# RWKV chunk solve: seven dependent 32-row steps per chunk, or a 128x128 inverse completed on TensorE and one product

## The chip, the cores and the metric

One core of a Trainium2 chip. The metric is the device time of one execution in microseconds, as the median of several runs.

## The reference, cut to what matters

Two transformer-like blocks on 256 tokens of width 2048. The first block mixes tokens by a Mamba-2 SSD on one half of the heads and by RWKV-7 on the other, then comes a cross-attention and an MLP; the second block has window attention, an S5 scan and a gated MLP. The RWKV-7 mixer, with 16 heads of 64, is the part at hand:

```
def step(state, inp):
    r_t, w_t, k_t, v_t, kk_t, a_t = inp
    sa = jnp.einsum('bhij,bhj->bhi', state, -kk_t)
    state = (state * w_t[:, :, None, :] + sa[..., None] * (kk_t * a_t)[:, :, None, :]
             + v_t[..., None] * k_t[:, :, None, :])
    return state, jnp.einsum('bhij,bhj->bhi', state, r_t)
```

Both kernels compute it in two chunks of 128 tokens. Inside a chunk the recurrence over `sa` becomes a unit lower triangular system of 128 unknowns per head: (I - G) z = b, with G strictly triangular.

## The kernel before, in words

All large products (`gemm`) stream fp32 weights from HBM in units of 1024 columns per partition. SyncE issues the loads; ScalarE rounds a unit to fp32r (`wh`), VectorE takes the rest (`wl`), and TensorE multiplies weight and activation halves in fp32r, into banks of the pool `mm` (four banks in this phase). The order of the large products is `w_in`, `wk`, `wv`, `w_outa`, `w_outb`, and so on.

Everything else is side work: Python generators that `step` resumes between groups of weight products. A hand-made meter (`Meter`) estimates the engines' time; a generator is resumed when its own time has come, so each `yield` is a hop of at least one group. What is emitted so is then ordered per engine by a planner that simulates the program; each engine works through its instructions in order. `step(True)` (forced) is called where a product needs a result of side work that is not there.

The RWKV side work of eight head pairs i (two heads in one 128-partition tile), in four quarters of two pairs:

- `rwkv_prep(i)`: scaled tiles `ka`, `be`, `al`, `rh`, `vt`, `bon` (pool `g`, 42 tiles) and `ga`, the masked 128x128 matrices G of two heads and two chunks. It holds back while `i > outs + LIVE`, where `outs` counts finished pairs.
- `rwkv_inv(q)`: GpSimd gathers the four 32x32 diagonal blocks of eight matrices (two pairs, two heads, two chunks), VectorE transposes them, GpSimd inverts all of them in 31 steps (tiles `T` and `W`), VectorE transposes the result into `Wc`. One at a time. Its tiles come from a pool of three.
- `rwkv_out(i)`, up to four at once: per chunk, products `gkp`, right side `b`, then the solve by forward substitution over four row blocks: the update `c` (from the second block on) and the product `z` with the block's inverse, each with its evacuation by VectorE and a `yield`; then state `s0` and result `y`. At the end it loads the second half of the pair's `lora` by SyncE into the tile `kbt` and writes its result into `bon`, which becomes `mix[8 + i]`.

The weight product `wv` has four blocks of two banks; `evac_v` writes four tiles per block, blocks 0 and 1 into the pool `m` (35 tiles), blocks 2 and 3 into the pool `g`. `w_outb` needs all of `mix`.

Of the kernel before, what the change touches and what calls it, by code (L numbers as in the profile page):

```python
# [13 lines left out]
AF = mybir.ActivationFunctionType  # L14
ALU = mybir.AluOpType
AX = mybir.AxisListType
P = 128
# [284 lines left out]
class Net:  # L302
# [116 lines left out]
    def step(self, force=False):  # L419

        mt, keep = self.meter, self.meter.t
        if force and self.sides:
            mt.clk["pe"] = max(mt.now(), min(e[0] for e in self.sides))
        for e in list(self.sides):
            if e[0] <= mt.now():
                mt.t = max(e[0], mt.now())
                try:
                    next(e[1])
                    e[0] = mt.t + e[2]
                except StopIteration:  # L430
                    self.sides.remove(e)
        mt.t = keep
# [267 lines left out]
    def rwkv_inv(self, qn, qd):  # L700

        nc = self.nc
        gp = nc.gpsimd
        iv = lambda n: self.ivp.tile([P, 1024], F32, tag="iv", name=f"{n}{qn}")
        Dt = iv("D")
        gp.memset(Dt, 0.0)
        d3 = Dt.rearrange("p (c h) -> p c h", h=32)
        for i in (2 * qn, 2 * qn + 1):
            for h in range(2):
                for q in range(4):  # L710
                    s = slice(32 * q, 32 * q + 32)
                    o = (i % 2) * 4 + 2 * h
                    gp.tensor_copy(d3[s, :, o:o + 2].rearrange("p c h -> p h c"),
                                   qd[i]["ga"][h].rearrange("p (c t) -> p c t", c=2)[s, :, 32 * q:32 * q + 32])
        for _ in range(3):
            yield
        L = iv("L")
        nc.vector.transpose(L, Dt)
        W = iv("W")
        T = self.ivp.tile([P, 256], F32, tag="ivt", name=f"T{qn}", bufs=1)  # L720
        nc.sync.dma_start(W, self.io["eye32"])
        w3 = W.rearrange("p (c i) -> p c i", i=32)
        for k in range(31, 0, -1):
            n = 32 - k
            t3 = T[:, :n * k].rearrange("p (c i) -> p c i", i=k)
            self.mul(t3, L[:, 32 * k:32 * k + k].unsqueeze(1).broadcast_to((P, n, k)),
                     w3[:, k:, k:k + 1].broadcast_to((P, n, k)), gp)
            self.add(w3[:, k:, :k], w3[:, k:, :k], t3, gp)
        for _ in range(13):
            yield  # L730
        Wc = iv("Wc")
        nc.vector.transpose(Wc, W)
        qd["wc"] = Wc.rearrange("p (c h) -> p c h", h=32)

    def rwkv_out(self, i, qd):
        nc = self.nc
        st = qd[i]
        ka, be, al, rh, vt, ga, nn, wc = (
            st["ka"], st["be"], st["al"], st["rh"], st["vt"], st["ga"], st["nn"], qd["wc"])
        hq = (i % 2) * 4  # L740

        yt = ka
        h64 = lambda h: slice(64 * h, 64 * h + 64)
        pt = self.pst(f"kt{i}")
        nc.tensor.transpose(pt[:, :P], ka[:, :P], self.ident)
        nc.tensor.transpose(pt[:, P:S], be[:, :P], self.ident)
        kbt = self.gp.tile([P, S], F32, tag="kb", name=f"kbt{i}", bufs=KB)
        self.act(kbt[:, :P], pt[:, :P], AF.Copy)
        self.mul(kbt[:, P:].rearrange("p (h j) -> p h j", h=2), pt[:, P:S].rearrange("p (h j) -> p h j", h=2),
                 nn[:, 0:2].unsqueeze(2).broadcast_to((P, 2, 64)))  # L750
        s0 = None
        for c in range(2):
            cc = slice(c * P, (c + 1) * P)
            gks = []
            pts = self.pst2(f"gkp{i}{c}")
            self.beside([(pts[h][:, n * P:(n + 1) * P], a[h64(h), cc], b[h64(h), cc], True, True)
                         for n, (a, b) in enumerate(((ka, rh), (ka, al), (be, rh))) for h in range(2)])
            for h in range(2):
                gk = self.t2(f"gk{i}{c}{h}")
                pt = pts[h]  # L760
                self.mul(gk[:, :S], pt[:, :S], self.c("mk"))
                self.stt(gk[:, S:3 * P], pt[:, S:3 * P], nn[:, 2 * c + h:2 * c + h + 1], self.c("mk", 0, P), ALU.mult, ALU.mult)
                gks.append(gk)
            yield
            pt = self.pst(f"b{i}{c}")
            if c:
                nc.tensor.matmul(pt[:, :P], al[:, cc], s0, start=True, stop=False)
            for h in range(2):
                nc.tensor.matmul(pt[:, h64(h)], gks[h][:, P:2 * P], vt[:, c * P + 64 * h:c * P + 64 * h + 64],
                                 start=c == 0, stop=c == 0 or h == 1)  # L770
            b, z = be[:, cc], al[:, cc]
            self.act(b, pt[:, :P], AF.Copy)
            yield
            for q in range(4):
                rows = slice(32 * q, 32 * q + 32)
                if q:
                    pt = self.pst(f"c{i}{c}{q}")
                    for h in range(2):
                        nc.tensor.matmul(pt[rows, h64(h)], ga[h][:32 * q, c * P + 32 * q:c * P + 32 * q + 32],
                                         z[:32 * q, h64(h)], start=True, stop=True)  # L780
                    self.add(b[rows], b[rows], pt[rows, :P])
                    yield
                pt = self.pst(f"z{i}{c}{q}")
                for h in range(2):
                    nc.tensor.matmul(pt[rows, h64(h)], wc[rows, :, hq + 2 * h + c], b[rows, h64(h)], start=True, stop=True)
                nc.vector.tensor_copy(z[rows], pt[rows, :P])
                yield
            if c == 0:
                pt = self.pst(f"s{i}")
                nc.tensor.matmul(pt[:, :P], kbt[:, P:], z, start=True, stop=False)  # L790
                nc.tensor.matmul(pt[:, :P], kbt[:, :P], vt[:, :P], start=False, stop=True)
                s0 = self.t(f"s0{i}")[:, :P]
                nc.gpsimd.memset(s0, 0.0)
                for h in range(2):
                    self.ts(s0[h64(h), h64(h)], pt[h64(h), h64(h)], st["sc"][h64(h)], None, ALU.mult)
            pt = self.pst(f"y{i}{c}")
            if c:
                nc.tensor.matmul(pt[:, :P], rh[:, cc], s0, start=True, stop=False)
            for h in range(2):
                o = pt[:, h64(h)]  # L800
                nc.tensor.matmul(o, gks[h][:, :P], vt[:, c * P + 64 * h:c * P + 64 * h + 64], start=c == 0, stop=False)
                nc.tensor.matmul(o, gks[h][:, S:3 * P], z[:, h64(h)], start=False, stop=c == 0 or h == 1)
            self.act(yt[:, cc], pt[:, :P], AF.Copy)
            yield
        lo = kbt
        nc.sync.dma_start(lo, self.io["lora"][i][:, S:])
        lws = self.split(lo, f"lorg{i}")
        bs = self.small(f"bs{i}", 24)
        mv = self.small(f"mv{i}", 8)
        for j in range(4):  # L810
            nc.vector.bn_stats(bs[:, 6 * j:6 * j + 6], yt[:, 64 * j:64 * j + 64])
        for j in range(4):
            nc.vector.bn_aggr(mv[:, 2 * j:2 * j + 2], bs[:, 6 * j:6 * j + 6])
        var = self.small(f"var{i}", 4)
        self.ts(var, mv.rearrange("p (j k) -> p j k", k=2)[:, :, 1], 64e-5, None, ALU.add)
        rs = self.rsqrt_small(var, 4, f"gn{i}")
        for j in range(4):
            y = yt[:, 64 * j:64 * j + 64]
            self.ts(y, y, mv[:, 2 * j:2 * j + 1], rs[:, j:j + 1], ALU.subtract, ALU.mult)
        yield  # L820
        pt = self.pst(f"yT{i}")
        for c in range(2):
            nc.tensor.transpose(pt[:, c * P:(c + 1) * P], yt[:, c * P:(c + 1) * P], self.ident)
        for a in range(2):
            self.hilo(pt[:, S:], [w[:, a * P:(a + 1) * P] for w in lws], self.pg[a], a == 0, a == 1)
        y3, bon = self.t(f"y3{i}"), st["bon"]
        self.act(y3, pt[:, :S], AF.Identity, scale=self.v("ln_w", i), bias=self.v("ln_b", i))
        self.add(bon, y3, bon)
        self.mul(bon, bon, pt[:, S:])
        y3 = bon  # L830
        self.mix[8 + i] = y3
        self.outs += 1
        yield
# [956 lines left out]
```

## Time and profile before

| | |
|---|---|
| median of 3 runs | 2951.19 us (2949.64 to 2951.55) |
| profiled execution | 2947.2 us, span 2945.4 us |
| busy: TensorE, VectorE, ScalarE, GpSimd | 2879.7, 2066.4, 1411.1, 350.7 us |
| matmul records | 19604 |

A busy TensorE is not TensorE at its peak: matmuls overlap, so what one costs is read from the distance between starts. Each fp32 matmul of the solve leaves two records. Nearly all instructions carry the line of one recording helper, so they are told apart by the tiles that they write and read (`z<-be,Wc` writes z and reads be and Wc). The granted clock is 1.0 at 2.4 GHz and 0.5 at 1.2 GHz.

### The profile page before, as it was taken

How to read it: one execution, taken by the hardware profiler on the slowest of the kernel's cores; microseconds unless marked ns; L12 is line 12 of the kernel's file. 1: busy time of each engine (PE TensorE's matmuls, PEld its weight loads, DVE VectorE, ACT ScalarE, POOL GpSimd, SP SyncE). 2: the span in 40 equal slices, each digit the busy share in tenths (PEclk: the TensorE clock that was granted, in tenths of full speed). 3: DMA queues.
4: the chain of work that ended last, by engine and by line, in shares of the span. 5: the costliest groups of instructions: out<-in, count | busy, mean ns of one | idle time of the engine just before them, and what ended most of it. 6: DMA issues, size and time to landing. Idle time of an engine off the chain costs nothing.

```text
span 2945.4 us, 50103 instructions
## 1 busy us (share of the span) xinstructions
PE 2879.7 (98%) x19604; PEld 2618.0 (89%) x19604; DVE 2066.4 (70%) x3761; ACT 1411.1 (48%) x2223; POOL 350.7 (12%) x574
## 2 busy tenths in 40 slices
PE   8989999989999999999999989999999999999998
PEld 7988998779999989988988989999988888888887
DVE  7978777567667675565566688897767765567755
ACT  6553543324554554455455544553554444444444
POOL 3446115600000000000000051210000000000000
PEclk9999999969999999999999999999999999999999
DMA  6544544416555666666656644545565566655664
GB/s 213 176 146 126 155 147 134 155 52 192 173 152 165 185 192 188 186 187 190 191 184 186 193 141 148 157 151 172 187 192 187 182 190 187 192 186 184 189 190 146
DMA packets 146252, 504.15 MB, mean 171 GB/s; under 512 B 16352, under 2 KB 24800, under 8 KB 146016
## 3 DMA queue, kind: packets, MB, share of 16 engines
q1 hardware_dynamic: 146016, 500.96, 54.6%
q8 instruction: 153, 2.51, 0.3%
q14 instruction: 83, 0.68, 0.1%
HBM read 498.80 MB, written 2.10 MB: 170 GB/s over the span
## 4 chain that ended last, share of the span: by engine, by line
PE 86%; POOL 7%; DVE 4%; issue 2%; ACT 1%; DMA 1%; SPq 0%; DVEq 0%; POOLq 0%; ACTq 0%
PE mm_w_up L266 17%; PE mm_w_in L266 12%; PE mm_w L266 12%; PE mm_w2a L266 5%; PE mm_w_db L266 4%; PE mm_w_da L266 4%; PE mm_w2c L266 4%; PE mm_w2b L266 4%; PE mm_wo L266 3%; PE mm_wq L266 3%; POOL T L266 3%; PE mm_w_out L266 3%; POOL W L266 3%; PE mm_wk L266 2%; PE mm_w_outa L266 2%
## 5 line engine op out<-in xcount | busy, mean ns | idle before, releaser
L266 PE MATMUL mm_w_up<-xu,wh_w_up 128*128 128x512 f32 x1408 | 487.9, 397 | 0.0
L266 PE MATMUL mm_w_up<-xu,wl_w_up 128*128 128x256 f32 x1408 | 376.6, 280 | 0.0
L266 PE MATMUL mm_w<-xf,wh_w 128*128 128x512 f32 x1024 | 350.6, 392 | 0.0
L266 DVE TENSOR_TENSOR wl_w_up<-raw_w_up,wh_w_up 128x1024 fp32r<-128x1024 f32 x176 | 215.4, 1224 | 148.2 <-ACT wh_w_up L266 147.4
L266 PEld LDWEIGHTS mm_w_up<-xu,wh_w_up 128*128 128x128 f32 x1408 | 256.9, 188 | 54.7
L266 ACT CAST wh_w_up<-raw_w_up 128x1024 fp32r<-128x1024 f32 x176 | 184.8, 1050 | 236.0 <-PE mm_w_up L266 220.8
L266 ACT CAST wh_w_in<-raw_w_in 128x1024 fp32r<-128x1024 f32 (+1 forms) x189 | 196.7, 1043 | 209.8 <-PE mm_w_in L266 121.1
L266 PE MATMUL mm_w_in<-ins,wh_w_in 128*128 128x256 f32 (+1 forms) x1248 | 288.9, 318 | 6.2 <-DVE ins L266 6.2
L266 DVE TENSOR_TENSOR wl_w_in<-raw_w_in,wh_w_in 128x1024 fp32r<-128x1024 f32 (+1 forms) x189 | 241.9, 1284 | 60.1 <-ACT wh_w_in L266 58.6
L266 PEld LDWEIGHTS mm_w_up<-xu,wl_w_up 128*128 128x128 f32 x1408 | 265.6, 189 | 9.8
L266 PE MATMUL mm_w<-xf,wl_w 128*128 128x256 f32 x1024 | 273.4, 280 | 0.0
L266 PE MATMUL mm_w_in<-xb,wh_w_in 128*128 128x256 f32 x1472 | 268.6, 284 | 1.1 <-DVE in L266 1.1
L266 DVE TENSOR_TENSOR wl_w<-raw_w,wh_w 128x1024 fp32r<-128x1024 f32 x128 | 156.8, 1225 | 122.1 <-ACT wh_w L266 120.5
L266 PEld LDWEIGHTS mm_w_in<-xb,wh_w_in 128*128 128x128 f32 x1472 | 226.8, 190 | 5.7 <-issue 2.3
L266 PEld LDWEIGHTS mm_w_in<-ins,wh_w_in 128*128 128x128 f32 x1248 | 208.8, 195 | 18.6 <-DVE ins L266 6.2
L266 PEld LDWEIGHTS mm_w<-xf,wh_w 128*128 128x128 f32 x1024 | 186.8, 188 | 35.9
L266 PE MATMUL mm_w_in<-ins,wl_w_in 128*128 128x256 f32 x768 | 216.2, 289 | 2.2 <-DVE wl_w_in L266 2.1
L266 PE MATMUL mm_w_in<-xb,wl_w_in 128*128 128x256 f32 x736 | 206.4, 284 | 2.1 <-DVE wl_w_in L266 2.1
L266 ACT CAST wh_w<-raw_w 128x1024 fp32r<-128x1024 f32 x128 | 134.3, 1049 | 144.4 <-PE mm_w L266 119.1
L266 PEld LDWEIGHTS mm_w<-xf,wl_w 128*128 128x128 f32 x1024 | 192.3, 188 | 7.0
L266 PEld LDWEIGHTS mm_w_in<-ins,wl_w_in 128*128 128x128 f32 x768 | 149.8, 195 | 6.8 <-DVE wl_w_in L266 3.8
L266 POOL TENSOR_TENSOR tt<-st,st 128x256 f32<-128x256 f32 x16 | 13.8, 860 | 1112.6 <-DVE acc L266 1111.8
(1504 smaller groups left out, 7501.9 us busy)
## 6 DMA issues: line engine op xcount, KB each, us to landing
raw_w_in<-in_w_in_dram SPq DMA_DIRECT2D x187, 512.0 KB, 3.6
raw_w_up<-in_w_up_dram SPq DMA_DIRECT2D x176, 512.0 KB, 3.8
raw_w<-in_w_dram SPq DMA_DIRECT2D x128, 512.0 KB, 4.2
raw_w2a<-in_w2a_dram SPq DMA_DIRECT2D x48, 512.0 KB, 3.9
raw_w_da<-in_w_da_dram SPq DMA_DIRECT2D x44, 512.0 KB, 4.0
raw_w_db<-in_w_db_dram SPq DMA_DIRECT2D x42, 512.0 KB, 3.9
raw_w2b<-in_w2b_dram SPq DMA_DIRECT2D x40, 512.0 KB, 4.2
raw_w2c<-in_w2c_dram SPq DMA_DIRECT2D x40, 512.0 KB, 4.2
```

The lines of the kernel that those rows point to most:

```text
L266: return f(o, *a, **k)
```

## The change

`rwkv_inv` goes on after `Wc`. It copies the blocks' inverses out (`Md`) and transposes them (`MdT`); then, for all eight matrices at once and in four stages with a `yield` between, TensorE forms the off-diagonal blocks: `ia` and `ib` those of 32x32 beside two diagonal blocks, `ic` and `id` the one of 64x64. ScalarE, VectorE and GpSimd copy the parts into two more tiles of the pool of three, `Q` and `M`; `M` ends as eight 128x128 inverses. `rwkv_out` then has one product per chunk and head (`inv` times `b`), one copy and one `yield` where it had seven steps. In `step`, a forced step now always advances the meter to the next time that lies ahead of it, where it stayed if some generator was due already.

```diff
--- before.py
+++ after.py
@@ -420,7 +420,7 @@
 
         mt, keep = self.meter, self.meter.t
         if force and self.sides:
-            mt.clk["pe"] = max(mt.now(), min(e[0] for e in self.sides))
+            mt.clk["pe"] = min([e[0] for e in self.sides if e[0] > mt.now()], default=mt.now())
         for e in list(self.sides):
             if e[0] <= mt.now():
                 mt.t = max(e[0], mt.now())
@@ -730,13 +730,54 @@
             yield
         Wc = iv("Wc")
         nc.vector.transpose(Wc, W)
-        qd["wc"] = Wc.rearrange("p (c h) -> p c h", h=32)
+
+
+        Q, M = iv("Q"), iv("M")
+        j3 = lambda a, n: a.rearrange("p (j c) -> p j c", c=n)
+        m3 = j3(M, P)
+        gp.memset(M, 0.0)
+        gp.memset(Q[:64, 512:], 0.0)
+        Md, MdT, Y1, Z64 = Q[:, :256], Q[:, 256:512], T, Q[:, 512:]
+        d, z64 = j3(Md, 32), j3(Z64, 64)
+        nc.vector.tensor_copy(d, Wc.rearrange("p (c h) -> p h c", h=32)[:, :8])
+        nc.vector.transpose(MdT, Md)
+        yield
+        blk = [slice(32 * q, 32 * q + 32) for q in range(4)]
+        lo, hi = slice(0, 64), slice(64, P)
+        gs = [qd[i]["ga"][h][:, c * P:(c + 1) * P] for i in (2 * qn, 2 * qn + 1) for h in range(2) for c in range(2)]
+        c32 = [slice(32 * j, 32 * j + 32) for j in range(8)]
+        c64 = [slice(64 * j, 64 * j + 64) for j in range(8)]
+        pts = self.pst2(f"ia{qn}")
+        self.beside([(pts[q // 2][blk[q + 1], c32[j]], gs[j][blk[q], blk[q + 1]], MdT[blk[q], c32[j]], True, True)
+                     for j in range(8) for q in (0, 2)])
+        self.act(Y1[blk[1]], pts[0][blk[1], :256], AF.Copy)
+        nc.vector.tensor_copy(Y1[blk[3]], pts[1][blk[3], :256])
+        for q in range(4):
+            self.act(m3[blk[q], :, blk[q]], d[blk[q]], AF.Copy)
+        for q in range(2):
+            gp.tensor_copy(z64[blk[q], :, blk[q]], j3(MdT, 32)[blk[q]])
+        yield
+        pts = self.pst2(f"ib{qn}")
+        self.beside([(pts[q // 2][blk[q], c32[j]], Y1[blk[q + 1], c32[j]], Md[blk[q + 1], c32[j]], True, True)
+                     for j in range(8) for q in (0, 2)])
+        self.beside([(pts[0][blk[1], c32[j]], Md[blk[1], c32[j]], Y1[blk[1], c32[j]], True, True) for j in range(8)])
+        self.act(z64[blk[1], :, blk[0]], j3(pts[0][blk[1], :256], 32), AF.Copy)
+        nc.vector.tensor_copy(m3[blk[0], :, blk[1]], j3(pts[0][blk[0], :256], 32))
+        nc.vector.tensor_copy(m3[blk[2], :, blk[3]], j3(pts[1][blk[2], :256], 32))
+        yield
+        pt = self.pst(f"ic{qn}")
+        self.beside([(pt[hi, c64[j]], gs[j][lo, hi], Z64[lo, c64[j]], True, True) for j in range(8)])
+        self.act(Z64[hi], pt[hi], AF.Copy)
+        yield
+        pt = self.pst(f"id{qn}")
+        self.beside([(pt[lo, c64[j]], Z64[hi, c64[j]], m3[hi, j, hi], True, True) for j in range(8)])
+        nc.vector.tensor_copy(m3[lo, :, hi], j3(pt[lo], 64))
+        qd["inv"] = m3
 
     def rwkv_out(self, i, qd):
         nc = self.nc
         st = qd[i]
-        ka, be, al, rh, vt, ga, nn, wc = (
-            st["ka"], st["be"], st["al"], st["rh"], st["vt"], st["ga"], st["nn"], qd["wc"])
+        ka, be, al, rh, vt, nn, inv = (st["ka"], st["be"], st["al"], st["rh"], st["vt"], st["nn"], qd["inv"])
         hq = (i % 2) * 4
 
         yt = ka
@@ -771,20 +812,11 @@
             b, z = be[:, cc], al[:, cc]
             self.act(b, pt[:, :P], AF.Copy)
             yield
-            for q in range(4):
-                rows = slice(32 * q, 32 * q + 32)
-                if q:
-                    pt = self.pst(f"c{i}{c}{q}")
-                    for h in range(2):
-                        nc.tensor.matmul(pt[rows, h64(h)], ga[h][:32 * q, c * P + 32 * q:c * P + 32 * q + 32],
-                                         z[:32 * q, h64(h)], start=True, stop=True)
-                    self.add(b[rows], b[rows], pt[rows, :P])
-                    yield
-                pt = self.pst(f"z{i}{c}{q}")
-                for h in range(2):
-                    nc.tensor.matmul(pt[rows, h64(h)], wc[rows, :, hq + 2 * h + c], b[rows, h64(h)], start=True, stop=True)
-                nc.vector.tensor_copy(z[rows], pt[rows, :P])
-                yield
+            pt = self.pst(f"z{i}{c}")
+            for h in range(2):
+                nc.tensor.matmul(pt[:, h64(h)], inv[:, hq + 2 * h + c], b[:, h64(h)], start=True, stop=True)
+            nc.vector.tensor_copy(z, pt[:, :P])
+            yield
             if c == 0:
                 pt = self.pst(f"s{i}")
                 nc.tensor.matmul(pt[:, :P], kbt[:, P:], z, start=True, stop=False)
```

## Rows read from the trace of the kernel before

**Rows 1.** page: busy us of TensorE; its clock per fortieth of the span

```profile
PE 2879.7 (98%) x19604; PEld 2618.0 (89%) x19604; DVE 2066.4 (70%) x3761; ACT 1411.1 (48%) x2223; POOL 350.7 (12%) x574
PEclk9999999969999999999999999999999999999999
```

**Rows 2.** stretches: us; busy PE, PEld, DVE, ACT, POOL; clock, DMA, GB/s

```profile
40.00:500.00 460.00, 443.89 (x3482) 413.84 (x3481) 369.89 (x786) 222.68 (x412) 182.67 (x306) 0.98 0.48 149
500.00:594.07 94.07, 91.08 (x473) 71.57 (x472) 56.22 (x107) 31.31 (x41) 47.13 (x74) 0.99 0.48 150
594.07:643.58 49.51, 44.36 (x286) 37.51 (x284) 29.77 (x128) 6.01 (x19) 0.00 (x0) 0.60 0.04 14
643.58:718.87 75.29, 75.29 (x548) 68.48 (x548) 54.30 (x124) 33.88 (x52) 0.00 (x0) 0.98 0.59 182
```

**Rows 3.** timeline of PE (start, us, what): solve steps of pair 4, first chunk

```profile
547.76 0.44 PE L266 MATMUL z<-be,Wc 32*32 32x64 f32 x4
...
551.64 0.41 PE L266 MATMUL c<-al,ga 32*32 32x64 f32 x4
...
587.84 0.38 PE L266 MATMUL s<-al,kbt 128*128 128x128 f32 x2
```

**Rows 4.** groups of PE, 594.07 to 643.58: count, busy us, mean ns, idle before

```profile
L266 PE MATMUL z<-be,Wc 32*32 32x64 f32 x72 | 9.8, 290 | 0.9 <-ACT be L266 0.7
...
L266 PE MATMUL c<-al,ga 32*32 32x64 f32 (+2 forms) x48 | 6.5, 289 | 0.4 <-DVE al L266 0.4
```

**Rows 5.** timeline of DVE: `wv` evacuations, and out 5's last row between

```profile
553.82 1.28 DVE L266 TENSOR_SCALAR v<-mm_wv,memy 128x256 f32<-128x256 f32 x3
...
624.95 0.41 DVE L266 TENSOR_TENSOR bon<-bon,yT 128x256 f32<-128x256 f32 x1
...
641.47 0.88 DVE L266 TENSOR_SCALAR v<-mm_wv,memy 128x256 f32<-128x256 f32 x2
```

**Rows 6.** chain of waits (start, us, what): `w_outb`, weight products alone

```profile
718.87 46.09 PE mm_w_outb L266 x384
```

**Rows 7.** timeline of PE: one z step among weight products

```profile
306.41 0.28 PE L266 MATMUL mm_w_in<-ins,wl_w_in 128*128 128x256 f32 x1
306.62 0.44 PE L266 MATMUL z<-be,Wc 32*32 32x64 f32 x4
306.98 0.50 PE L266 MATMUL mm_w_in<-ins,wh_w_in 128*128 128x256 f32 x2
307.32 0.28 PE L266 MATMUL mm_w_in<-ins,wl_w_in 128*128 128x256 f32 x1
```

**Rows 8.** timeline of PE: z and c interleaved (first of seven rows), what follows

```profile
309.93 0.26 PE L266 MATMUL z<-be,Wc 32*32 32x64 f32 x1
...
310.30 0.39 PE L266 MATMUL mm_w_in<-ins,wl_w_in 128*128 128x256 f32 x1
```

**Rows 9.** timeline of PE: four `b` records and what follows

```profile
302.72 0.56 PE L266 MATMUL b<-vt,gk 128*128 128x64 f32 x4
303.12 0.39 PE L266 MATMUL xt<-cst,xbc 128*128 128x128 f32 x2
```

**Rows 10.** groups of the whole span: the solve steps on PE and DVE

```profile
L266 PE MATMUL z<-be,Wc 32*32 32x64 f32 x256 | 29.7, 247 | 0.9 <-ACT be L266 0.7
...
L266 PE MATMUL c<-al,ga 32*32 32x64 f32 (+2 forms) x192 | 21.1, 239 | 3.2 <-DVE al L266 3.2
...
L266 DVE COPY al<-z 32x128 f32<-32x128 f32 x64 | 18.3, 286 | 20.8 <-PE z L266 17.7 <-PE c L266 1.9
...
L266 DVE TENSOR_TENSOR be<-be,c 32x128 f32<-32x128 f32 x48 | 13.8, 287 | 18.6 <-PE c L266 16.8 <-PE z L266 0.8
```

**Rows 11.** waits, 40 to 719: who for whom, us, times, longest us

```profile
PE st L266 <- DVE xe L266: 7.0, 1, 7.0
...
PE c L266 <- DVE al L266: 3.2, 2, 2.8
...
DVE Wc L266 <- POOL W L266: 22.8, 4, 7.8
```

## The prediction

> **What bounds the kernel now.** I read the page first: TensorE is busy 98% of the span, and the slices of its granted clock show one dip, to 0.6, in the ninth [rows 1]. So time can only come from what TensorE executes, from the places where it stands still, and from that dip. Only about the first 720 us hold the RWKV work, so next I read busy times by stretch [rows 2]. From 40 to 594 us TensorE idles 19 us in 554 and runs near its full clock; 594.07 to 643.58 differs: a mean clock of 0.60 (of the two levels, 2.4 GHz at 1.0 and 1.2 GHz at 0.5, it is mostly at the lower), ScalarE 6.0 us busy, and 14 GB/s of weights where 149 to 182 flow around it. Its 44.4 us of TensorE are stretched by the clock and hold little work. The stretch after it is dense again. Call it the hole: 49.5 us without the weight product `wv`, save two records.
>
> Why is it there? In it run the outs of head pairs 4 to 7, a step at a time [rows 4]. The solve of one chunk is seven products that follow each other, each resumed only when the hand-made meter steps the side work: for pair 4 the first stands at 547.76, the second at 551.64, and the product behind the seventh at 587.84, so 40 us for seven hops [rows 3]. Meanwhile block 1 of `wv` has evacuated three of its four tiles at 553.82; the next ones come only at 641.47, after outs 4 and 5 have written their last rows (the second at 624.95) [rows 5]. By the code, blocks 2 and 3 of `evac_v` take tiles of the pool `g`, 42 in all: four finished results, eight for each of four open pairs, and the split second loads of `lora` (two tiles each) leave none. So block 2 sits in PSUM, block 3 has no bank, and TensorE has nothing but the serial solve. The link from pool to wait is inferred; the times are read.
>
> **Part 1: small products that go, outside the hole.** All z and c groups together are 256 and 192 records [rows 10], two per matmul, four per step. The hole holds 72 and 48 [rows 4], so 328 records, 82 steps, stand among weight products. What a step costs there is read from the starts around one: alone, 384 records of 256 columns take 46.09 us, 0.12 from start to start [rows 6]. Here the weight record at 306.41 is followed by z at 306.62 (0.09 late), z by the next pair at 306.98 (0.36), and that pair takes 0.34 for 0.24 (0.10 late) [rows 7]. Sum 0.55. **82 x 0.55 = 45 us go.**
>
> **Part 2: the hole.** If the outs need one hop where they needed seven, outs 4 and 5 save six hops of about 5.7 us in the first chunk alone, 34 us before the hole begins, and the pairs before them save too, which opens preparations 5 to 7 (held back by `outs + LIVE`) and the next inverse earlier. They would be through before block 2 needs tiles. Then the hole's other 164 records (286 less 120 and two of `wv`) run among weight products; four `b` records take 0.40 us [rows 9], 0.10 each, so 16 us. **49.5 - 16.4 = 33 us go.** Ends: 42, if they pack as in [rows 8] (0.046 each); 16, if the hole stays and loses only the busy time of its z and c (9.8 + 6.5, [rows 4]).
>
> **Part 3: the one product.** 16 groups of two 128-row matmuls with 64 columns, four records, like `b`: 0.40 [rows 9] and 0.19 for going in and out [rows 7]. **16 x 0.6 = 10 us come.**
>
> **Part 4: completing the inverse.** Per quarter 56 matmuls, 112 records: `ia` 32 and the first half of `ib` 32, alternating between two disjoint row groups; 16 each in the second half of `ib`, `ic` and `id`, all on one row group. For the first kind the row is z and c interleaved: eight records from 309.93 to 310.30, 0.046 each [rows 8]. For the second, z alone, 0.36 for four [rows 7], 0.09 each. So 64 x 0.046 + 48 x 0.09 + 5 insertions x 0.19 = 2.9 + 4.3 + 1.0 = 8.2 us, **33 us come in four quarters.** Ends: 25, if all pack; 62, if every four records pay the whole 0.55.
> The Trainium skill ("TensorE: Matmul & The Clock Gate", Part 3: Packing small matmuls) says that a weight load overlaps running matmuls only where the row group differs, which speaks against `ic`, `id` and half of `ib`. The two prices just read, 0.046 and 0.09, agree. Its span model, some 4 ns for each further tile, would put `ia` and the first half of `ib` near 0.4 us each where I take 1.5; as an estimate from that page the forecast would be 9 us lower.
>
> **Part 5: waits.** VectorE waits in all four quarters for GpSimd's last W, 22.8 us in sum, because it is in line behind the transpose [rows 11]. What is queued behind it is the splitting of weights, and TensorE pays later: 7.0 in its longest wait, 3.2 in others. Now `d`, its transpose and `ia` stand right behind that transpose, and TensorE is itself in order: behind `ia` are weight products. Nothing in the trace shows a TensorE wait directly on the inverse. Bounds: minus 10 (today's waits of 7.0 and 3.2 go) to plus 28 (four of 7.0). Steps that wait for an evacuation today lose little: 3.2 us in all c groups [rows 11], 0.9 in all z groups [rows 10]; so I take **1 us per quarter, 4 us come.**
>
> **At nothing.** VectorE loses 112 small operations, 32.1 us [rows 10], and gets 16 copies of like size and per quarter five small copies and a transpose, some 3 us (an estimate from 0.29 for 128 columns); ScalarE gets seven small copies, GpSimd two memsets and two copies per quarter. GpSimd is idle in half of 500 to 594 [rows 2], VectorE is under 81% from 40 to 500; if that cover failed it would show in the fourth rival. No DMA is added; each out's second `lora` load moves forward in SyncE's queue with its out, and weights behind it wait less. The line in the forced step changes only the order of emission; it also acts after 767 us, and I put plus or minus 3 us on it, an estimate: it can act only where a product waits for side work, and TensorE idles 66 us in the whole span (2945.4 - 2879.7, [rows 1]).
>
> **Sum:** -45 - 33 + 10 + 33 + 4 = -31. The profiled execution (2947.2 us, span 2945.4) would come to 2916; it lies 4 us under the median of the runs shown, so of 2951.2 I make **2920 us**.
>
> **Rivals.**
> (a) The hole stays. `g` tiles bind later too, or the planner puts the outs no earlier. For: at 641.47 the evacuation came 16 us after the last row of out 5, so the freed tile was not all [rows 5]. Against: 40 us per solve is so much the longest item. Then -45 - 16 + 10 + 33 + 4 = -14: 2937 us.
> (b) More than forecast: all stages pack (25 for 33) and today's waits of 10 us go where I add 4: -45 - 33 + 10 + 25 - 10 = -53: 2898 us. For: the first kind of stage packs already; VectorE gets lighter, so the queues behind the transpose are shorter.
> (c) Slower. TensorE's queue stops at the inverse: `ia` is placed where the planner expects W, W is late as it is in four of four quarters, and `ib`, `ic`, `id` each wait for copies on two loaded engines while weight products stand behind. At 7.0 for `ia` and 2.8 (the larger of c's two waits, [rows 11] for their sum) for three stages this is 15.4 us per quarter, 62 in all, in place of 4: +27, 2978 us. It decides from 9 us per quarter on, where the other terms (-35) are used up. Against: z and c stages, built alike, wait 4 us over 448 records.
> (d) It doesn't do what it says: the chain gets shorter but VectorE takes over as the bound. All of 40 to 719 holds 510 us of VectorE [rows 2]; the outs of 500 to 700 pulled into a stage that is 80% full would starve the weight products. If TensorE's idle 16 us of 40 to 500 doubled, and as much came in 500 to 594, it is 30 us back: 2950 us.
>
> **Chances.** Forecast 0.55 (own range 2905 to 2937), (a) 0.13, (b) 0.17, (c) 0.10, (d) 0.05. About 0.2%, 6 us, is what a measurement of this kernel tells from no change; some of (a) and of the dear end of part 4 fall within it: faster 0.82, same 0.07, slower 0.11. The range leaves out (c), part of (d), and what of (b) and of the bounds goes beyond 2893: 2893 to 2947.
>
> **What would show it.** No stretch of 40 us or more without weight products and at a clock near 0.6 before `w_outb`; `wv` blocks 1 to 3 evacuated in turn; `w_outb` begins near 687 instead of 719. z as 64 records of 128 rows; 448 records in `ia` to `id` at 0.05 to 0.1 us from start to start. VectorE's wait for W still four times. Wrong would be: TensorE waits on `ia` to `id` over 9 us per quarter, or the hole moved elsewhere with another pool full.

## The result, and the profile after

The changed kernel takes 2920.1 us (median of 4 runs, 2918.8 to 2921.0) against 2951.4 of the kernel before on the same chip; the ratio is 0.9895, with a 95% interval of 0.9877 to 0.9912. That is 31 us, or 1.05%, less. The forecast was 2920, so its sum came out. Its terms didn't all: this part of the document is mostly about that. One of the ten executions of a run further down (the stages issued three times) took 6831.9 us and is left out of that run's median.

The profiled execution of the changed kernel has a span of 2917.7 us, 27.7 less than before. The page, as in [rows 1], gives busy time, and the granted clock per fortieth of the span:

```profile
PE 2840.0 (97%) x19668; PEld 2598.8 (89%) x19668; DVE 2037.5 (70%) x3689; ACT 1423.4 (49%) x2251; POOL 357.4 (12%) x590
...
PEclk9999999999999999999999999999999999999999
```

TensorE is busy 39.7 us less (2879.7 before), with 64 records more. The dip of the clock in the ninth slice is gone.

The stretches of [rows 2], cut at the same times, in the changed kernel (columns as there: us; busy PE, PEld, DVE, ACT, POOL; clock, DMA share, GB/s), and under them the last part cut finer:

```profile
40.00:500.00 460.00, 434.57 (x3626) 413.54 (x3627) 362.18 (x793) 236.24 (x443) 187.51 (x321) 0.97 0.47 149
500.00:594.07 94.07, 88.04 (x477) 72.91 (x478) 52.59 (x94) 31.27 (x42) 48.63 (x76) 0.96 0.45 146
594.07:643.58 49.51, 49.51 (x408) 44.78 (x408) 34.52 (x81) 24.53 (x36) 0.00 (x0) 1.00 0.64 203
643.58:718.87 75.29, 71.37 (x575) 69.29 (x575) 52.88 (x143) 30.90 (x58) 0.00 (x0) 0.93 0.38 125
...
680.00:700.00 20.00, 16.08 (x104) 15.24 (x103) 12.84 (x59) 6.54 (x16) 0.00 (x0) 0.76 0.20 61
```

Three things are to be seen here. The hole is filled: 594 to 644 has TensorE busy throughout, at full clock, and 203 GB/s of weights. TensorE idles more before it: 25.4 us of 40 to 500 (16.1 before), 6.0 of 500 to 594 (3.0 before). And a new gap stands where none was: 680 to 700, clock 0.76, 61 GB/s.

What that gap is, the chain of waits shows (start, us, what):

```profile
691.79 0.64 PE mm_w_outb L266 x3
692.43 0.65 PE yT L266 x3
693.10 2.63 DMA xin<-in_x_dram
695.82 0.43 DVE xin L266
696.30 40.73 PE mm_w_outb L266 x321
```

The product `w_outb` took 46.09 us in one piece before [rows 6]. Now its first record is at 676.8 and 63 of the 384 go early, but the other 321 run from 696.30, behind the ends of outs 6 and 7 (their last `bon` rows start at 690.3 and 696.2, their last products on TensorE, `yT`, stand in this chain): 60 us from its first to its last record. In the gap TensorE falls to the lower of its two clock levels: behind 692.4 its records start 0.21 us apart, where 0.12 is usual. The very last release is a tile `xin`, loaded only at 693.10. It is the eighth of sixteen: by the code it lies in the pool `m`, and in the built program it takes the place of a tile that the products `yT` of every out read, up to the last. So this load waits for out 7 too, and SyncE's waits show it (who for whom: us, times, longest):

```profile
SPq L1548 <- PE yT L266: 8.0, 1, 8.0
```

The end of `w_outb` moved from 764.96 (718.87 + 46.09) to 737.03 (696.30 + 40.73), 27.9 us earlier, about the whole change of the span. So everything that the change did to the time it did before 740 us.

The inverse of the first quarter on TensorE, in its timeline (start, us, what), and one product of the solve with what follows it:

```profile
217.91 0.69 PE L266 MATMUL ia<-Q,ga 32*32 32x32 f32 x32
218.53 0.38 PE L266 MATMUL mm_w_in<-ins,wh_w_in 128*128 128x256 f32 x1
...
230.89 0.60 PE L266 MATMUL ib<-Q,T 32*32 32x32 f32 x26
...
231.92 0.38 PE L266 MATMUL pb<-qh,bonesr 128*128 128x256 f32 x1
...
242.78 1.14 PE L266 MATMUL ic<-Q,ga 64*64 64x64 f32 x16
243.85 0.39 PE L266 MATMUL mm_w_in<-ins,wh_w_in 128*128 128x256 f32 x1
...
248.07 1.14 PE L266 MATMUL id<-M,Q 64*64 64x64 f32 x16
...
263.69 0.55 PE L266 MATMUL z<-be,M 128*128 128x64 f32 x4
264.08 0.61 PE L266 MATMUL b<-vt,gk 128*128 128x64 f32 x4
```

From the start of a stage to the start of what follows: `ia` 0.62 us for 32 records, `ib` 1.03 for 48, `ic` 1.07 for 16, and `id` the same 1.1. That is 3.8 us, with some 0.2 for going in and out of each stage 4.6 us a quarter, where the forecast had 8.2.

The waits from 40 to 719 us (who for whom: us, times, longest), as in [rows 11]:

```profile
DVE Wc L266 <- POOL W L266: 38.8, 4, 11.9
...
PE b L266 <- DVE gk L266: 20.8, 3, 8.9
...
PE st L266 <- DVE xe L266: 7.7, 1, 7.7
```

VectorE waits 16 us more for GpSimd's W, and a wait of TensorE is new: `b`, the right side of a chunk, for `gk`. VectorE's timeline shows why (in brackets: idle before, and what ended it):

```profile
570.45 1.25 DVE L266 STREAM_TRANSPOSE Wc<-W 128x1024 f32<-128x1024 f32 x1 [10.57 <-POOL W L266]
571.61 1.18 DVE L266 TENSOR_TENSOR wl_wv<-raw_wv,wh_wv 128x1024 fp32r<-128x1024 f32 x1
572.72 0.41 DVE L266 TENSOR_TENSOR gk<-gkp,cst 128x256 f32<-128x256 f32 x1
...
573.19 1.28 PE L266 MATMUL b<-vt,gk 128*128 128x64 f32 x4 [6.03 <-DVE gk L266]
```

VectorE stands 10.57 us for W, everything behind the transpose is late by that, `gk` among it, and TensorE, which is in order as well, stands 6.03 us at `b` (the last row is TensorE's). Each of the four waits for W has such a wait of TensorE behind it: `st` at 175.2 (7.7 us), `b` at 305.5, 451.0 and 573.2 (5.9, 8.9, 6.0), 28.5 us in sum. And each costs more than it lasts: behind it TensorE goes on for a while at the lower of its two clock levels (columns of the stretches as above):

```profile
175.00:179.00 4.00, 3.78 (x19) 3.81 (x20) 4.00 (x9) 3.80 (x9) 1.71 (x3) 0.56 0.55 168
305.50:308.00 2.50, 2.50 (x15) 2.38 (x17) 2.50 (x7) 1.07 (x4) 0.00 (x0) 0.50 0.03 7
451.00:454.00 3.00, 3.00 (x14) 3.00 (x15) 2.09 (x5) 0.28 (x1) 0.62 (x1) 0.50 0.10 10
573.20:577.00 3.80, 3.80 (x19) 3.18 (x19) 3.80 (x8) 0.28 (x1) 0.00 (x0) 0.50 0.62 174
```

In the first of them the records start 0.21 us apart up to 178.5, which loses some 1.3 us (an estimate: 2.9 us of records at 0.21 in place of 0.12).

### The profile page after: what moved, and what is told of

Same layout as the page of the kernel before. It is cut to its first block, busy times and chain, and to the rows that moved or that the text cites. A ratio compares the mean times of both kernels' runs of the same rounds, so it can differ in the third digit from the quotient of the medians.

```text
span 2917.7 us, 50239 instructions
## 1 busy us (share of the span) xinstructions
PE 2840.0 (97%) x19668; PEld 2598.8 (89%) x19668; DVE 2037.5 (70%) x3689; ACT 1423.4 (49%) x2251; POOL 357.4 (12%) x590
## 4 chain that ended last, share of the span: by engine, by line
PE 78%; DVE 3%; POOL 1%; issue 1%; ACT 0%; DMA 0%; DVEq 0%; ACTq 0%; POOLq 0%
PE mm_w_up L266 17%; PE mm_w L266 12%; PE mm_w_in L266 7%; PE mm_w2a L266 5%; PE mm_w_db L266 4%; PE mm_w_da L266 4%; PE mm_w2c L266 4%; PE mm_w2b L266 4%; PE mm_wo L266 3%; PE mm_wq L266 3%; PE mm_w_out L266 3%; PE mm_wv L266 2%; PE mm_w_outa L266 2%; PE mm_w_outb L266 2%; PE mm_w_ba L266 2%; PE mm_wk L266 1%
```

## The experiments

The kernel before took 2949.1 to 2950.1 us (medians) beside the runs that follow, and 2951.4 beside the changed kernel: differences between runs of different sets are good to some 2 us. Unless it is said otherwise, times are medians of three rounds.

### The forced step, and ga held longer

The one line in the forced step, put into the kernel before:

```diff
-            mt.clk["pe"] = max(mt.now(), min(e[0] for e in self.sides))
+            mt.clk["pe"] = min([e[0] for e in self.sides if e[0] > mt.now()], default=mt.now())
```

> The kernel before with the one new line of the forced step and nothing else. The prediction put it at nothing, plus or minus 3 us: 2951, between 2948 and 2954. A rival reading of the result, that part of the 31 us is owed to this line because it moves the outs, expects 2940 or less.

Measured: 2950.2, ratio 1.0001 (0.9991 to 1.0010). The line is worth nothing in the kernel before, as the prediction had it. In the changed kernel it was not taken out by itself; what follows puts everything down to the inverse and the solve.

To test why the hole went, the tiles `ga` were to be kept until the second chunk's solve:

```diff
             nc.vector.tensor_copy(z, pt[:, :P])
             yield
+            if c:
+                for h in range(2):
+                    nc.gpsimd.tensor_copy(self.small(f"hold{i}{h}", 1), st["ga"][h][:, :1])
```

> The changed kernel with the tiles ga held until the second chunk's solve of each pair (a one-column read of each on GpSimd there), as long as the kernel before held them; the solve stays one product. Theory A, the reason that the prediction gave (the stretch without weight products went because the outs end sooner): no change, 2920, within 3 us. Theory B (it went because ga, two tiles of the pool g per pair, now comes free at the inverse): block 2 of wv is evacuated only after the solves of pairs 4 and 5, some 10 us later than at 589 to 597, and part of the stretch is back: 2928 to 2940.

Measured: 2919.1, no change. But the trace says that the edit didn't hold anything. GpSimd's timeline (idle before in brackets):

```profile
98.58 0.18 POOL L266 COPY hold<-ga 128x1 f32<-128x1 f32 x1 [17.43 <-DVE ga L266]
```

The read of pair 0 ran at 98.58 us, right behind the write of `ga` and 170 us ahead of its solve: the planner moved it up, since it depends on nothing later. So this run decides nothing between the two theories.

### The old solve on top of the inverse

Two kernels keep the completed inverse but solve in seven products again. In one, the coupling blocks come from the inverse and `ga` stays free early; in the other they come from `ga`, as before, which so is really held. The first is there for its time alone: blocks of the inverse are not those of G, so it doesn't solve the system. The core of both edits (the second has `ga` in place of the slice of `inv`):

```diff
-            pt = self.pst(f"z{i}{c}")
-            for h in range(2):
-                nc.tensor.matmul(pt[:, h64(h)], inv[:, hq + 2 * h + c], b[:, h64(h)], start=True, stop=True)
-            nc.vector.tensor_copy(z, pt[:, :P])
-            yield
+            for q in range(4):
+                rows = slice(32 * q, 32 * q + 32)
+                if q:
+                    pt = self.pst(f"c{i}{c}{q}")
+                    for h in range(2):
+                        nc.tensor.matmul(pt[rows, h64(h)], inv[:32 * q, hq + 2 * h + c, 32 * q:32 * q + 32],
+                                         z[:32 * q, h64(h)], start=True, stop=True)
+                    self.add(b[rows], b[rows], pt[rows, :P])
+                    yield
+                pt = self.pst(f"z{i}{c}{q}")
+                for h in range(2):
+                    nc.tensor.matmul(pt[rows, h64(h)], inv[rows, hq + 2 * h + c, rows], b[rows, h64(h)], start=True, stop=True)
+                nc.vector.tensor_copy(z[rows], pt[rows, :P])
+                yield
```

> The changed kernel, its inverse kept, but the solve again in seven products of 32 rows, whose coupling blocks are read from the inverse in place of ga (so the output differs from the reference); ga still comes free at the inverse. Both theories: 96 steps come back at 0.55 us, +53. Theory A: the outs end about 70 us later, the stretch without weight products is back, +33 more, 3006, with block 2 of wv evacuated after the last rows of outs 4 and 5. Theory B: block 2 of wv is evacuated before outs 4 and 5 end, no gap between its tiles, 2973, plus whatever the late outs 6 and 7 make w_outb wait.

> The changed kernel with the old solve: seven products per chunk with ga as coupling, the inverse completed and its diagonal blocks used. Against the kernel before it has the inverse alone. Prediction's terms 4 and 5: 2951 + 33 + 4 = 2988. Reading of the changed kernel's trace (4.6 us a quarter on TensorE, waits 12 to 16 us): 2951 + 18 + 14 = 2983 with the stretch as long as before; if the later inverse lengthens the stretch without weight products too, by up to its 78 us of added delay, over 3000.

Measured: 2953.2 and 2950.7. Both expectations were 20 us and more too high, and the reason is instructive. Here is the second kernel, with seven steps and `ga` held: the stretch of the hole (columns as above), VectorE's timeline, and the chain at the end.

```profile
594.07:643.58 49.51, 46.97 (x351) 40.79 (x350) 39.05 (x79) 21.77 (x35) 19.03 (x31) 0.97 0.57 181
```

```profile
591.64 0.86 DVE L266 TENSOR_SCALAR v<-mm_wv,memy 128x256 f32<-128x256 f32 x2
595.68 0.48 DVE L266 TENSOR_SCALAR v<-mm_wv,memy 128x256 f32<-128x256 f32 x1
...
651.59 0.42 DVE L266 TENSOR_TENSOR bon<-bon,yT 128x256 f32<-128x256 f32 x1
...
722.94 0.42 DVE L266 TENSOR_TENSOR bon<-bon,yT 128x256 f32<-128x256 f32 x1
```

```profile
723.08 1.04 PE mm_w_outb L266 x7
728.86 34.82 PE mm_w_outb L266 x288
```

There is no hole, although the outs of pairs 4 and 5 end at 651.59 us and later, 26 us and more behind the kernel before [rows 5], and 60 us behind the first evacuation of block 2. **Theory A falls**: block 2 of `wv` doesn't need short outs. **Theory B falls as well**, as the only cause: `ga` is held here. The addresses in the built programs show the link that the prediction had inferred from the code. Each of the four tiles of block 2 takes over the place of another tile of the pool `g`:

| kernel | block 2's four tiles take the places of | hole |
|---|---|---|
| before | second load of pair 1, `ga` of pair 5, `be` of pairs 4 and 5 | yes |
| changed | first load of pair 7 (two), `ga` of pair 4 (two) | no |
| seven steps, `ga` free early | second load of pair 3 (two), `ga` of pair 4 (two) | no |
| seven steps, `ga` held | second load of pair 3 (two), finished results of pairs 0 and 1 | no |

In the kernel before, three of four wait for the solves of pairs 4 and 5. In the others they don't. With the inverse in it the outs lie elsewhere relative to `wv`, and the planner finds tiles that are free. Why it found none before isn't settled by these runs.

And filling the hole was no gain by itself. In the kernel with `ga` held, what came in there is lost again at `w_outb`, which lasts from 685.4 to 763.7 us, waiting for outs 6 and 7 (last row at 722.94). The serial chain of the RWKV work has to be over before `w_outb` can be; where TensorE waits for it is a matter of order.

### Hops without products, and stages three times

```diff
             nc.vector.tensor_copy(z, pt[:, :P])
             yield
+            for _ in range(6):
+                yield
```

> The changed kernel with six empty hops behind each solve's one product: the hops of the seven-step solve without its products. If the 33 us that the seven steps cost are the length of the chain (outs 6 and 7 end at 730 in place of 696, and w_outb waits for them), 2945 to 2953 and the steps themselves cost nearly nothing; if they are the products among the weight products, 2920 and 33/96 = 0.34 us a step; in between, the share is read from how far outs 6 and 7 end later.

Measured: 2926.4, 6 us more; outs 6 and 7 end at 697.8 and 704.6, 8 us later. Six empty hops per chunk are cheap: of the 33 us between one product and seven (2953.2 less 2920.1), 6 are hops. The rest lies with the steps themselves; that it is their way through TensorE's queue and VectorE's is an inference.

```diff
-        self.beside([(pt[hi, c64[j]], gs[j][lo, hi], Z64[lo, c64[j]], True, True) for j in range(8)])
+        self.beside([(pt[hi, c64[j]], gs[j][lo, hi], Z64[lo, c64[j]], True, True) for j in range(8)], 3)
```

(and so for all stages; `beside` issues its list as often as it is told)

> The changed kernel with the matmuls of ia to id issued three times over (the same products into the same places): 896 more records at the same places, no wait more. The prediction's price (0.046 and 0.09 a record, 7.2 us a quarter and copy): +58, 2978. The price that the changed kernel's trace shows (3.8 us a quarter and copy): +30, 2950.

Measured: 2952.4, so 32 us for two further copies in four quarters, 4.0 a quarter and copy. The trace's price of 3.8 holds, the prediction's 7.2 doesn't. `ic` and `id` last 3.01 us each in the first quarter of this trace. It isn't a pure price, since the outs come later as well (outs 6 and 7 end at 725 and 728). But TensorE doesn't idle more for it: 31.7 us from 40 us to the end of `w_outb` (727.1 less 695.4 busy), 35.4 in the changed kernel (697.0 less 661.6). That leaves no room for double the price.

The stage `ib` of this trace has both kinds of 32 x 32 products behind each other, first those that alternate between two row groups, then those on one (timeline of TensorE):

```profile
242.86 1.61 PE L266 MATMUL ib<-Q,T 32*32 32x32 f32 x90
244.29 0.21 PE L266 MATMUL ib<-T,Q 32*32 32x32 f32 x1
...
244.41 1.58 PE L266 MATMUL ib<-T,Q 32*32 32x32 f32 x45
245.92 0.38 PE L266 MATMUL mm_w_in<-ins,wh_w_in 128*128 128x256 f32 x1
```

From start to start that is 0.016 us a record (90 in 1.43) against 0.034 (45 in 1.51).

### The transpose of W in its place

The program has the transpose of W one hop ahead of `ia`. The planner has VectorE take it 38 to 47 us ahead of `ia`, and VectorE waits there. One line keeps it in its place:

```diff
-        nc.vector.transpose(Wc, W)
+        self.tc.keep_in_program_order(nc.vector.transpose(Wc, W))
```

> The changed kernel with the transpose of W kept at its program place in VectorE's queue, some 40 us later than where it waits for GpSimd now. If the waits of the inverse cost what the trace shows (VectorE 38.8 us for W, and behind it TensorE's b 20.8 us for gk): 2900 to 2910. If these waits are covered, or the time is only lost elsewhere: 2920.

Measured: **2885.3**, ratio 0.9782 (0.9768 to 0.9797), 35 us less than the changed kernel. The wait of VectorE for W and that of `b` for `gk` are both gone from the list of waits. It is 15 us and more beyond what was expected of the waits listed for `b`: `st` no longer waits either, TensorE's idle time from 40 us to the first record of `w_outb` falls by 24 us (636.8 - 605.3 = 31.5 before this edit, 604.1 - 596.9 = 7.2 with it), and its mean clock there rises from 0.97 to 0.99. The stretches at the lower clock behind the four waits are gone as well: at these places (160 to 200 us, 280 to 320, 400 to 440, 530 to 560) the clock is 1.00. The same line in the kernel before, and in the kernel with inverse and old solve (`ga` held):

> The kernel before with the transpose of W kept at its program place on VectorE, nothing else. It tells whether the 35 us that this gave in the changed kernel were lost by the change or were there before it. If they go with the waits (22.8 us on W before, 38.8 after): 35 x 22.8 / 38.8 = 21, 2930. If the change alone made them dear (its b stands behind gk, gk behind the transpose): 2945 to 2951.

> The changed kernel with the old solve (seven products, coupling from ga) and the transpose of W in program order: no VectorE wait on W in it. Against the changed kernel with the transpose in order (2885) it prices the solve: by the prediction's 0.55 a step and 96 steps 2938; by what seven steps cost before this edit (33) 2918. Against the kernel before with the same edit it prices the inverse: by the prediction +37, by the trace and by the threefold stages about +17.

Measured: 2927.0 (ratio 0.9925, 0.9908 to 0.9941) and 2936.9 (0.9959, 0.9945 to 0.9974). So the kernel before lost 22 us to the same waits, and the changed kernel loses 35: **the change made these waits some 12 us dearer.** (8.0 us of waiting for W remain in the kernel before under this line, and 9.0 in the third kernel, where none was expected; so their gains may be a little short.) The third kernel gains only 14 (2950.7 to 2936.9), and without the line it waits 20.6 us for W, no more than the kernel before. So it isn't the inverse that made the waits dear, but the one product behind it; how wasn't taken apart.

These three kernels are free or nearly free of that disturbance, and so tell the two halves of the change apart: the inverse alone costs 10 us (2927.0 to 2936.9), the one product in place of seven gives 52 (2936.9 to 2885.3). With the waits in place the same two steps were 1 and 31 (2950.0, 2950.7, 2920.1): the parts depend on one another. The 2936.9 is what the price of 0.55 a step foretold, 2938, but not for that reason, as the starts and ends of `w_outb` show below. The hole is still in the first of them. Its stretch there (columns as above), and VectorE's timeline:

```profile
575.00:622.00 47.00, 42.95 (x281) 35.74 (x279) 25.68 (x110) 5.11 (x17) 0.00 (x0) 0.69 0.08 28
```

```profile
543.95 0.48 DVE L266 TENSOR_SCALAR v<-mm_wv,memy 128x256 f32<-128x256 f32 x1
...
622.20 0.88 DVE L266 TENSOR_SCALAR v<-mm_wv,memy 128x256 f32<-128x256 f32 x2
```

By the spans of the three profiled executions:

| with the transpose in order | kernel before | inverse added, old solve | one product |
|---|---|---|---|
| `w_outb` begins | 699.3 | 679.9 | 644.1 |
| `w_outb` ends | 745.5 | 753.3 | 701.8 |
| it takes | 46.2 | 73.4 | 57.7 |

Adding the inverse brings the start of `w_outb` 19 us forward, although it puts 18 us (4 x 4.6) on TensorE: the hole goes, worth at most some 37. At most, because 15 of the 112 steps (60 of 448 records of z and c) now run behind the start of `w_outb`, and so are put off and not saved. `w_outb` is stretched by 27. The one product then brings its start 36 us forward, and takes 16 of the 27 back.

### The late outs

If `w_outb` is stretched by late outs, an earlier inverse must help. The program lets 13 hops pass between W and the transpose:

```diff
-        for _ in range(13):
+        for _ in range(7):
             yield
```

> The changed kernel with 7 empty hops in place of 13 between the emission of W and that of the inverse's completion: ia to id come some 34 us earlier, W is there by then in three of four quarters. If the late end of outs 6 and 7 (696 us) is what stretches w_outb from 46 to 60 us: outs end 20 to 35 us earlier and 2906. If another wait ends last there: 2920. If ia now stands in TensorE's queue before W is ready, the prediction's rival (c): 2930 or more.

Measured: 2906.3 (ratio 0.9849, 0.9835 to 0.9864), 14 us less, as expected. Outs 6 and 7 end at 634 and 638, some 57 us earlier where 20 to 35 were expected, and `w_outb` is dense again. Both edits together, with 11 hops and with 9:

> The changed kernel with the transpose of W in program order and 11 empty hops before it in place of 13: W is ready 12 us before it in quarter 2 and 21 us in quarter 3, so two hops fit. If the late outs 6 and 7 still stretch w_outb (58 us where 46 is dense): outs 12 us earlier or more, 2873 to 2879. If not: 2885.

> The same with 9 hops: the outs another 12 us earlier, but the transpose now stands where W is not ready in two or three quarters. If the outs still end last: 2870 to 2874, w_outb dense. If the waits on W come back in VectorE's queue: above the kernel with 11 hops, 2880 to 2890.

Measured: **2875.5** (0.9754, 0.9739 to 0.9768) and 2876.5 (0.9754, 0.9740 to 0.9769). The chain of waits with 11 hops has `w_outb` in one piece:

```profile
645.87 46.09 PE mm_w_outb L266 x384
```

That is the 46.09 of [rows 6], to the digit. The 10 us between 2885.3 and 2875.5 are what is left of the stretch. From 11 to 9 hops nothing is won, and neither range expected for 9 was met: with outs that no longer end last (647.7 with 11 hops, 2 us into `w_outb`, and 640.1 with 9, ahead of it), their place costs nothing. The version with 11 hops beats the kernel before by 74 us and the changed kernel by 45.

## Why the prediction was right, and where its steps were wrong

The sum was right, -31 against -31, by luck: errors of about equal size cancelled. The terms, as forecast and as the runs show them (the measured ones hold if the parts add up, and come from the three kernels with the transpose in order and from the traces):

| term | forecast | measured | from |
|---|---|---|---|
| solve steps less the one product | -45 + 10 = -35 | -36 | start of `w_outb`, 679.9 to 644.1 |
| the hole | -33 | -37 | 699.3 to 679.9, less 18 of inverse |
| the inverse | +33 | +18 | 4 x 4.6, stages issued three times |
| these three together | -35 | -55 | start of `w_outb`, 699.3 to 644.1 |
| waits | +4 | +12.6 | 34.8 less 22.1 |
| `w_outb` waits for outs 6 and 7 | not in the sum | +11.5 | 57.7 less 46.2 |
| sum | -31 | -31 | |

Only the line of the three together is a measurement as it stands. Its split is loose: the price of the inverse cancels against the hole's, and the forecast's hole has the thirty steps that run in it gone, while the measured one keeps them (they go in the first row). So what is shown is this: the start of `w_outb` came 20 us further forward than the three terms had it, and `w_outb` itself and the waits took these 20 us back.

**Part 1.** The sum is near; its price and its count aren't. With no hole, the steps in it run among weight products too. In the kernel with inverse and old solve, transpose in order, 97 steps stand ahead of `w_outb` (388 records of z and c); in the kernel with one product, 14 products stand there (56 records of z). So the 35.8 us are 0.43 for each of the 83 that go, not 0.55. The row on which the price stood [rows 7] is one step alone. Some of the steps of two pairs stand together, as in this timeline of TensorE in the kernel with inverse and old solve, transpose in order:

```profile
262.55 0.40 PE L266 MATMUL mm_w_in<-ins,wh_w_in 128*128 128x256 f32 x2
262.88 0.42 PE L266 MATMUL z<-be,M 32*32 32x64 f32 x8
263.23 0.38 PE L266 MATMUL mm_w_in<-ins,wl_w_in 128*128 128x256 f32 x1
263.45 0.40 PE L266 MATMUL mm_w_in<-ins,wh_w_in 128*128 128x256 f32 x2
```

By the working of the prediction this is 0.09 late, 0.35, 0.10 late: 0.54, but for two steps. Whether that is the whole difference wasn't counted out.

**Part 2.** The size can't be compared row by row (above); the reason is wrong. The hole didn't go because six hops fewer bring the outs through in time: with seven steps it is gone too. The forecast "34 us before the hole begins" didn't come about either: outs 4 and 5, of which it was made, start their last rows at 603.8 and 615.9, 19 and 9 us earlier than before, and outs 6 and 7 at 690.3 and 696.2, against 691.8 and 698.0. What the solve saves, the inverse takes: from the transpose of W to the last copy of `id` it is 68 to 92 us in the four quarters, and no out of the quarter can start its solve before that. The prediction priced `ia` to `id` in TensorE time and not in time along the chain; that is the step that failed here. That the pool `g` is the link holds.

**Part 3.** 0.39 us from `z` to what follows and some 0.1 for going back make 0.5, near the 0.6 of the forecast.

**Part 4.** The mechanism was right and its price twice too high. The 0.046 us a record [rows 8] came from `z` and `c` rows; `ia`, which alternates between two row groups, takes 0.62 us for 32, 0.019 each. On one row group it is 0.067 for 64 x 64 (`ic`, 1.07 for 16), where 0.09 was taken. The Trainium skill ("TensorE: Matmul & The Clock Gate", Part 3: Packing small matmuls) says that a weight load overlaps only where the row group differs; the trace agrees, with 0.016 against 0.034 for products of the same size, 32 x 32, in the stages issued three times. The estimate that the prediction made from the span model on that page of the Trainium skill, 0.4 us for `ia`, was nearer to the 0.62 than the prediction's own 1.5. The lower bound from rows, 25 us, didn't hold the 18.

**Part 5.** This term was mis-sized by some 9 us, though its upper bound (28) holds it. The prediction looked for the price at the inverse's own products. They hardly wait: no wait of TensorE on `ia` to `id` reaches half a microsecond. The price is where the prediction said that it is paid today, behind the transpose of W in VectorE's queue, and it grew, because new waits for W met a `gk` that TensorE needs at once. It read the old wait of 22.8 us as worth 7.0 + 3.2 on TensorE; the run without it shows 22.

**What is late next** was asked for the hole and not for the end. `w_outb` needs all eight finished results, and the last outs end where they ended; so a kernel that gets to `w_outb` 42 us earlier (718.9 to 676.8) must wait there. The row of the last `bon` was in the trace of before, at 698.0.

**The rivals.** (a) didn't come: no stretch of 40 us lacks weight products. (b) came in half: the stages cost 18, less than its 25, but the waits grew. (c) has the right kind of wait at another place: not at `ia` but at `b`, 12 us in all and not 62. (d) didn't come; where TensorE idles 25 us of 40 to 500, VectorE is 79% busy (362 of 460) and stands still itself, waiting for W.

Of the signs, the hole, the turn of `wv`'s blocks (but for the last tile of block 1), 64 records of `z` and the four waits for W came out; `w_outb` began earlier than the 687 foretold, and ended later than 687 + 46; the records of `ia` to `id` are mostly cheaper than the 0.05 us that was the lower end.

## What to carry to other kernels

A serial chain beside a full engine has one deadline, the first product that needs its last result; read from the trace when the chain ends and ask of each edit whether that moves, because a gap that is filled further up comes back there. An instruction that waits at the head of an in-order queue costs what stands behind it, so price such a wait by what the other engines need from that queue, or by a run that puts the instruction where its input is ready: here one line was worth more than the whole change, 35 us on top of its 31. And a sum that comes out is no proof of its terms; only the runs that undo one part at a time told them apart.

## What the hardware showed that was not expected

Records of small fp32 matmuls of 32 rows and 32 columns that alternate between two row groups start 0.016 to 0.019 us apart (90 in 1.43 us, 32 in 0.62); of the same size on one row group, 0.034 (45 in 1.51 us); 64 x 64 ones on one row group, 0.067 (16 in 1.07 us). Going from 128-row products to such a group and back costs about 0.2 us in all, whether four, eight or 32 records stand in it; and eight records of two solve steps take 0.35 us where four of one take 0.36, so that two steps side by side cost as much as one.
